# Two begun products of four pairs in place of two plain feature tiles at the start of the second feed forward

## The chip, the cores and the metric

One Trainium2 chip, one of its cores. The metric is the device time of one execution in microseconds; three executions of the kernel before gave 1340.26, 1340.63 and 1341.62 us, median 1340.63. Engines are named as in the profile: PE is TensorE (PEld its weight load), DVE is VectorE, ACT is ScalarE, POOL is GpSimd, SP is SyncE, whose queue issues the transfers. "Start" of an instruction is its place in the timeline, in us from the first instruction of the profiled execution.

## The reference

A decoder layer on 512 tokens of width 1024, all in fp32: a feed forward, token mixing, and a second feed forward. Only the last seam matters here.

```
def swiglu(x, w_gu, w_down):
    g, u = jnp.split(x @ w_gu, 2, axis=-1)
    return (jax.nn.silu(g) * u) @ w_down
...
h = h + rmsnorm(y, mix_post_w[l])                     # y: token mixing, y @ w_out
h = h + 0.5 * rmsnorm(swiglu(rmsnorm(h, ffn2_pre_w[l]), ffn2_w_gu[l], ffn2_w_down[l]), ffn2_post_w[l])
```

`w_gu` has 2 x 2816 columns: 22 feature tiles of 128 gate columns (g) and 128 up columns (u).

## The kernel before

**Numbers in two parts.** PE multiplies in a fast fp32 form. Each operand is split into a high part (`hi`, a rounding by ACT) and a low part (`lo`, the rest, a subtraction by DVE), and each product is three matmuls: hi·hi, hi·lo, lo·hi. So every weight piece of 128x512 elements costs one ACT and one DVE instruction before PE can use it (`split`, `wsplit`).

**Plain tiles and pairs.** The transposed, normalized tokens lie in `xhi[0]`, `xhi[1]` (the two halves of the 1024 inputs) with their low parts. The 512 tokens are four tiles t = 0..3 of 128; tiles 0 and 1 are the first token half, 2 and 3 the second. A plain feature tile (`gu_plain`) takes gate and up columns as they are: 8 slices x 3 matmuls x 2 column sets x 2 token halves = 96 matmuls with 256 moving columns. A pair (`pair`) takes the same gate and up columns as a 2 x 2 block product (input halves by token halves) with seven products in place of eight. Each product (`product`) is 12 matmuls of 256 columns, 84 in all. It pays for this on DVE. On the weight side there are sums s1, s2, s4 (a fourth, s3, is made by an accumulating transfer). On the token side there are the combinations t1..t4, made once by `combine`, which needs tile t of the second half with tile t - 2 of the first. Which operand a product needs:

```
self.xop = {1: q(0, 0), 2: q(1, 0), 3: q(1, 1), 4: self.xc["t4"], 5: self.xc["t1"], 6: self.xc["t2"], 7: self.xc["t3"]}
```

Products 1 and 2 read only the first token half; 3 reads the second half; 4 to 7 read the combinations t4, t1, t2, t3, which need both halves.

**The seam.** `out_proj` multiplies by `w_out` token tile by token tile, and per tile does the post norm (square on ACT, row factor `v` on DVE, power on POOL, two updates of h on DVE) and spawns `prenorm`: squares, factor, two scalings on DVE (line 204 before, 207 after), eight PE transposes into `px`, the splits into `xhi`, `xlo`, copies of the transposes kept for `combine`, and for t >= 2 `combine` itself. Tile 3 is the last, so its scaling ends the post norm chain of the whole seam.

Before, `ffn` of the second feed forward takes f = 0 and f = 1 as plain tiles (`early2=2, plain2=2`). It does both in the first token half, then one product of the pair f = 2 (`pair_begin`), and then both in the second token half. Then come the pairs, 20 of them, f = 2..21, with the `down` products of finished features between them (from f = 2 on, since the first chunk of `CHUNKS2` is 2 features).

**What sets the order.** The code is written in one order; a list scheduler places each engine's instructions by its own estimates, within dependences and pool sizes (18 split weights `w`, 5 `sum`, 4 `st`, 2 `sh`, 5 PSUM banks `ps`, 3 `px`). Each engine then works its own list strictly in order, and so does the SP queue. In names, the number behind a tile is its buffer.

Of the kernel before, what the change touches and what calls it, by code (L numbers as in the profile page):

```python
# [45 lines left out]

LAT = dict(comb=1.0, mem0=3.5, mem1=8.0, mem2=1.5, hg=1.5, hgx=6.0, hg1=6.0, hg2=11.0, hg3=6.0, hg4=6.0, dil0=4.0, exp=2.0, dil1=9.0, dil2=5.0,
           dil3=3.0, norm=8.0, mnorm=5.0, mload=10.0, start=0.1, step=2.0, keep=2.0)
PLAN = dict(early1=2, plain1=2, early2=2, plain2=2)
HALVES = (slice(0, 512), slice(512, 1024))  # L50


class Layer:
# [3 lines left out]
    def __init__(self, ctx, tc):  # L57
        self.tc, self.nc = tc, tc.nc
        nc = self.nc
        pool = lambda n, b, **k: ctx.enter_context(tc.tile_pool(name=n, bufs=b, **k))  # L60
        self.const = pool("const", 1)
        self.wpool = pool("wpool", NW)
        self.stage = pool("stage", NST)
        self.res = pool("res", 1)
        self.slots = pool("slots", NSLOT)
        self.small = pool("small", 4)
        self.ps = pool("ps", 5, space=PSUM)
        self.px = pool("px", 3, space=PSUM)
# [22 lines left out]
        self.ordered = 0  # L91

        self.strict = False

# [118 lines left out]
    def prenorm(self, src, gain, t, lat, raw):  # L213


        nc = self.nc
        ts = slice(t * P, (t + 1) * P)
        pts = []

        def keep(hf):  # L220
            raw[t, hf] = self.slot((P, 4, P))
            nc.scalar.copy(raw[t, hf], pts[hf])

        wait = self.strict and t < 2
        for x in self.normed(src, gain, lat, self.psum if self.strict and t == 1 else self.paux):
            if isinstance(x, float):
                yield x
                continue
            hf = len(pts)
            pts.append(x)  # L230
            self.split(self.xhi[hf][:, :, ts], self.xlo[hf][:, :, ts], x)
            if not wait and (t < 2 or hf == 0):
                keep(hf)
        if wait:
            def later():
                yield LAT['keep']
                keep(0)
                keep(1)
            self.spawn(later())
        if t < 2:  # L240
            return
        yield from self.combine(t, raw, pts, lat == LAT['norm'] and t == 2)
# [67 lines left out]
                out += [(hi[:, i, :], lo[:, i, :]) for i in range(per)]  # L310
        return out

    def wops(self, w, c1, c2, by_load):

        st = self.load(w, 0, KD, c1, P)
        a11, a12 = st[:, 0:4, :], st[:, 4:8, :]
        a22 = self.stage.tile([P, 4, P], F32, tag="st2", bufs=2, name=f"sh{self.uid()}")
        quarter = lambda h: w.rearrange("(k p) c -> p k c", p=P)[:, 4 * h:4 * h + 4, c2:c2 + P]  # L320
        self.bring(a22, quarter(1))
        sums, ops = {}, {}

        def new_sum():
            return self.wpool.tile([P, 4, P], F32, tag="sum", bufs=NSUM, name=f"sum{self.uid()}")

        if "s1" not in by_load:
            a21 = sums["a21"] = new_sum()
            self.bring(a21, quarter(0))
        for n, x in (("s1", a22), ("s3", a11)):  # L330
            if n in by_load:
                u = new_sum()
                self.bring(u, quarter(0))
                self.nc.gpsimd.dma_start(out=u, in_=x, accum_op=ALU.add)
                sums[n] = u
# [24 lines left out]
        def operand(j):  # L360
            if j not in ops:
                if j == 6:
                    total("s4")
                ops[j] = self.wsplit({1: a11, 2: a12, 4: a22}.get(j) if j in (1, 2, 4) else total({3: "s4", 5: "s1", 6: "s2", 7: "s3"}[j]))
            return ops[j]
        return get

    def pairs(self, specs, by_load=lambda i: ()):
# [24 lines left out]
    def product(self, out, ops, j, first=True):  # L393
# [3 lines left out]
        for k in range(4):  # L397
# [2 lines left out]
            mm(out, lhsT=lh, rhs=rl, start=False, stop=False, skip_group_check=True)  # L400
            mm(out, lhsT=ll, rhs=rh, start=False, stop=k == 3, skip_group_check=True)  # L401
            self.tick(3 * 0.1095)

    def pair_begin(self, ops):

# [179 lines left out]
    def ffn(self, w_gu, w_down, w_post, ready, reload, after, chunks, early, plain, last=False):  # L585


        nc = self.nc
# [4 lines left out]
        pairs = self.pairs([(w_gu, f * P, DFF + f * P) for f in range(plain, NF)], lambda i: ("s1", "s3")[i < 4:])  # L593

        def swiglu(sg, su, act):
            nc.scalar.activation(sg, sg, AF.Silu)
# [1 line left out]
            self.split(act[0], act[1], sg)  # L598

        def gu(ops, act):  # L600
            a, u, c, d, v = self.pair(ops)
            sg, su = self.slot(), self.slot()
            nc.scalar.copy(sg[:, :HT], a)
# [37 lines left out]
        if not resumed:  # L641
            self.open(ready, gw, uw, new_act, gu_mm, gu_act, heads, early)
            tasks = [[], ready.tasks]
        else:
            tasks.append(ready[0]())
        for i in range(early if resumed else 0):
            heads.append([[next(gw), next(uw)], new_act()])
            if i == 0:
                tasks.append(ready[1]())
        for i in range(early if resumed else 0):  # L650
            for j in range(2):
                if i == 0:
                    self.need(tasks[0][j])
                heads[i][0][j] = self.wcol(heads[i][0][j], i >= 2)
        self.strict = False
        begun = None
        for i in range(2):
            if i == 1 and resumed:
                begun = self.pair_begin(next(pairs))
            self.need(*tasks[i])  # L660
            for w, act in heads if i or resumed else ():
                gu_plain(w, act, slice(i * HT, (i + 1) * HT))
        f0, before, ws = 0, None, []
        for n in chunks:
            act = []
            for j in range(n):
# [6 lines left out]
                else:  # L673
# [610 lines left out]
def layer_kernel(ctx, tc, a, nbias, hmask, out):  # L1284
# [59 lines left out]
    def store(h, t):  # L1344
        for c, n in ((0, 512), (512, 256), (768, 256)) if t == NT - 1 else ((0, 512), (512, 512)):
# [2 lines left out]

    h1, h2 = spill("h1"), spill("h2")
    ready = L.ffn(a["ffn1_w_gu"][0], a["ffn1_w_down"][0], a["ffn1_post_w"][0], Source,  # L1350
                  reload(lambda t, hf: x[t * P:(t + 1) * P, HALVES[hf]]), follow(h1, a["mix_pre_w"][0]), CHUNKS1, PLAN['early1'], PLAN['plain1'])
    z = L.mixing(a, ready, nbias)
    ready = L.out_proj(z, a["w_out"][0], a["mix_post_w"][0], reload(lambda t, hf: h1[t][hf]), follow(h2, a["ffn2_pre_w"][0]))
    L.ffn(a["ffn2_w_gu"][0], a["ffn2_w_down"][0], a["ffn2_post_w"][0], [lambda: ready[:2], lambda: ready[2:]], reload(lambda t, hf: h2[t][hf]), store, CHUNKS2, PLAN['early2'], PLAN['plain2'], True)


def constants():
# [39 lines left out]
```

## Time and profile before

| What | Value |
|---|---|
| median of 3 executions | 1340.63 us (1340.26 to 1341.62) |
| span of the profiled execution | 1338.3 us; of its own time the page gives no other number |
| PE busy | 1326.2 us, 99% of the span |
| DVE, ACT, POOL busy | 78%, 56%, 7% |
| granted TensorE clock, mean | 0.999 |
| end of `out_proj` on PE / first plain product | 984.69 us |
| first matmul of what is left of pair f = 2 | 1010.30 us |

The span runs from the first to the last instruction; the median of the timed executions is 2.3 us above it. A busy PE is told from the starts of matmuls: their shown durations overlap.

### The profile page before, as it was taken

What the parts mean: (1) busy time and instruction counts of PE and PEld (TensorE: products, weight loads), DVE (VectorE), ACT (ScalarE), POOL (GpSimd) and SP (SyncE); (2) the same over time, 40 slices, a digit from 0 to 9 for tenths busy, and PEclk for the clock granted to TensorE, in tenths of its full rate; (3) what the DMA queues carried; (4) which work ended last, traced back from release to release, by engine and by line L of the source; (5) the groups of instructions that cost most, each with busy time, mean ns of one, the idle gap of its engine ahead of it and who ended that gap; (6) DMA issues with size and microseconds to landing.
All of it is one profiled execution on the core that took longest, in us unless ns stands there. A gap on an engine that the chain in (4) does not pass through costs nothing.

```text
span 1338.3 us, 24332 instructions
## 1 busy us (share of the span) xinstructions
PE 1326.2 (99%) x9228; PEld 1234.5 (92%) x9228; DVE 1044.0 (78%) x1979; ACT 754.1 (56%) x1557; POOL 87.3 (7%) x116
## 2 busy tenths in 40 slices
PE   9999999999999999999999999999999999999997
PEld 8999999999898988899899999999899999999996
DVE  7987777687897975699769968898588877777765
ACT  7764554465566764455665755566366644445541
POOL 1011110010100000000000000000011111111100
PEclk9999999999999999999999999999999999999999
DMA  9586556565525335334223333334645766555513
GB/s 252 150 203 164 144 147 166 126 161 184 166 66 158 111 95 177 121 106 127 64 80 111 112 87 96 103 98 150 202 111 158 187 164 154 142 143 155 145 64 126
DMA packets 238611, 183.14 MB, mean 137 GB/s; under 512 B 11129, under 2 KB 200990, under 8 KB 238494
## 3 DMA queue, kind: packets, MB, share of 16 engines
q1 hardware_dynamic: 223702, 159.49, 39.7%
q0 software_dynamic: 10368, 18.88, 8.5%
q10 hardware_dynamic: 4424, 3.22, 0.8%
q8 instruction: 72, 1.18, 0.4%
q14 instruction: 45, 0.37, 0.1%
HBM read 153.21 MB, written 9.47 MB: 122 GB/s over the span
## 4 chain that ended last, share of the span: by engine, by line
PE 65%; DVE 2%; DMA 1%; ACT 0%; issue 0%; POOLq 0%; DVEq 0%; ACTq 0%
PE ps L381 17%; PE ps L399 12%; PE ps L400 12%; PE ps L401 12%; PE px L381 7%; PE px L386 4%; PE px L390 1%; DVE w L168 1%; DVE s L168 0%; DMA sh<-in_w_in_dram 0%; DMA sum<-in_w_in_dram 0%; DVE s L736 0%; DVE s L1042 0%; DVE st L992 0%; ACT s L832 0%
## 5 line engine op out<-in xcount | busy, mean ns | idle before, releaser
L173 ACT ACTIVATE w<-sum 128x512 fp32r<-128x512 f32 x288 | 180.5, 631 | 208.6 <-PE ps L400 180.3
L168 DVE TENSOR_TENSOR w<-sum,w 128x512 fp32r<-128x512 f32 x288 | 197.0, 687 | 79.6 <-ACT w L173 77.6
L400 PE MATMUL ps<-xlo,w 128*128 128x256 f32 x864 | 245.0, 284 | 0.0
L399 PE MATMUL ps<-xhi,w 128*128 128x256 f32 x864 | 244.9, 283 | 0.0
L401 PE MATMUL ps<-xhi,w 128*128 128x256 f32 x864 | 244.5, 283 | 0.0
L173 ACT ACTIVATE w<-st 128x512 fp32r<-128x512 f32 x240 | 150.2, 630 | 119.0 <-PE ps L400 87.7
L168 DVE TENSOR_TENSOR w<-st,w 128x512 fp32r<-128x512 f32 x248 | 168.6, 687 | 33.6 <-ACT w L173 30.8
L381 PE MATMUL px<-s,s 128*128 128x512 f32 x816 | 193.0, 390 | 0.0
L168 DVE TENSOR_TENSOR s<-s,s 128x256 f32<-128x256 f32 (+3 forms) x317 | 176.5, 562 | 13.8 <-ACT s L173 3.1
L381 PEld LDWEIGHTS px<-s,s 128*128 128x128 f32 x816 | 150.6, 188 | 29.9 <-DVE s L168 0.4
L399 PEld LDWEIGHTS ps<-xhi,w 128*128 128x128 f32 x864 | 165.5, 192 | 2.1
L400 PEld LDWEIGHTS ps<-xlo,w 128*128 128x128 f32 x864 | 165.5, 192 | 2.0
L401 PEld LDWEIGHTS ps<-xhi,w 128*128 128x128 f32 x864 | 165.5, 192 | 0.0
L168 DVE TENSOR_TENSOR sum<-sum,st 128x512 f32<-128x512 f32 x176 | 120.2, 686 | 7.0 <-DMA st<-in_w_in_dram 2.5
L168 DVE TENSOR_TENSOR s<-s,ps 128x256 f32<-128x256 f32 (+1 forms) x195 | 93.0, 477 | 28.2 <-PE ps L381 22.2
L399 PE MATMUL ps<-t3hi,w 128*128 128x256 f32 x288 | 82.9, 288 | 0.0
L399 PE MATMUL ps<-t1hi,w 128*128 128x256 f32 x288 | 82.2, 285 | 0.0
L399 PE MATMUL ps<-t4hi,w 128*128 128x256 f32 x288 | 82.2, 285 | 0.0
L400 PE MATMUL ps<-t4lo,w 128*128 128x256 f32 x288 | 81.9, 284 | 0.0
L400 PE MATMUL ps<-t3lo,w 128*128 128x256 f32 x288 | 81.8, 284 | 0.0
L401 PE MATMUL ps<-t1hi,w 128*128 128x256 f32 x288 | 81.5, 283 | 0.0
L400 PE MATMUL ps<-t2lo,w 128*128 128x256 f32 x288 | 81.5, 283 | 0.0
(198 smaller groups left out, 2965.8 us busy)
## 6 DMA issues: line engine op xcount, KB each, us to landing
st<-in_ffn_w_gu_dram SPq DMA_DIRECT2D x48, 512.0 KB, 4.8
st<-in_w_in_dram SPq DMA_DIRECT2D x48, 512.0 KB, 3.7
st<-in_ffn_w_down_dram SPq DMA_DIRECT2D x44, 512.0 KB, 4.0
sum<-in_ffn_w_gu_dram SPq DMA_DIRECT2D x80, 256.0 KB, 3.3
sh<-in_ffn_w_gu_dram SPq DMA_DIRECT2D x40, 256.0 KB, 3.3
sum<-st POOLq DMA_DIRECT2D x40, 256.0 KB, 3.4
sum<-sh POOLq DMA_DIRECT2D x32, 256.0 KB, 3.6
sum<-in_w_in_dram SPq DMA_DIRECT2D x32, 256.0 KB, 3.0
```

What stands on the lines that cost most here:

```text
L168: ins = self.nc.vector.tensor_tensor(out=out, in0=a, in1=b, op=op)
L173: self.pin(self.nc.scalar.activation(hi, src, AF.Copy))
L381: self.pin_pe(mm(out, lhsT=lhs[l], rhs=rhs[r], start=a, stop=b))
L386: self.nc.tensor.matmul(out, lhsT=lhsT, rhs=rhs, start=start, stop=stop, **k)
L390: self.pin_pe(self.nc.tensor.transpose(out, in_, self.ident))
L399: mm(out, lhsT=lh, rhs=rh, start=first and k == 0, stop=False, skip_group_check=True)
L400: mm(out, lhsT=lh, rhs=rl, start=False, stop=False, skip_group_check=True)
L401: mm(out, lhsT=ll, rhs=rh, start=False, stop=k == 3, skip_group_check=True)
```

## The change

The second feed forward has no plain tile any more (`early2=0, plain2=0`), so all 22 features are pairs. In the first token half it does products 1 and 2 of the first four pairs (`begun2=4`, `pairs_begin`, in groups of two), each pair keeping its result of product 1 (`cp`) and of 1 + 2 (`sg`, the first half of the gate). When the second half comes, `pair_rest` does the five others in the order 7, 5, 6, 3, 4. The weights of the four pairs are loaded in two steps: at first only the 8 slices of gate columns (`st`), and the up columns (`sh`, and twice into `sum`, one of them with the accumulating transfer) when `more` is called. Since no plain tile reads the first input half of the second token half, that split (`xhi[0]`, `xlo[0]` of t = 2, 3) is left out (`whole`). The first feed forward has `begun1=0` and the same instructions as before.

```
-PLAN = dict(early1=2, plain1=2, early2=2, plain2=2)
+PLAN = dict(early1=2, plain1=2, begun1=0, early2=0, plain2=0, begun2=4)
...
-            self.split(self.xhi[hf][:, :, ts], self.xlo[hf][:, :, ts], x)
+            if self.whole or t < 2 or hf == 1:
+                self.split(self.xhi[hf][:, :, ts], self.xlo[hf][:, :, ts], x)
...
+    def pairs_begin(self, group):
+        out = []
+        for ops in group:
+            a, cp = self.psum((P, HT)), self.slot()
+            self.product(a, ops, 1)
+            self.nc.scalar.copy(cp[:, :HT], a)
+            out.append((ops, cp, self.slot(), a))
+        for ops, cp, sg, a in out:
+            self.product(a, ops, 2, False)
+            self.nc.scalar.copy(sg[:, :HT], a)
+        return [x[:3] for x in out]
+
+    def pair_rest(self, ops, cp):
...
+        c, d, b = (self.psum((P, HT)) for _ in range(3))
+        self.product(d, ops, 7)
+        nc.scalar.copy(p7, d)
+        self.product(c, ops, 5)
+        nc.scalar.copy(v, c)
+        self.product(b, ops, 6)
+        self.tt(u, cp[:, :HT], b, ALU.add)
+        self.tt(v, p7, v, ALU.subtract)
+        self.product(c, ops, 3, False)
+        self.product(d, ops, 4, False)
+        return u, c, d, v
...
+        first = [self.wops(w_gu, f * P, DFF + f * P, ("s3",), True) for f in range(plain, plain + begun)]
+        pairs = self.pairs([(w_gu, f * P, DFF + f * P) for f in range(plain + begun, NF)], lambda i: ("s1", "s3")[i < 4 - begun:])
...
-        begun = None
+        half = []
         for i in range(2):
-            if i == 1 and resumed:
-                begun = self.pair_begin(next(pairs))
             self.need(*tasks[i])
             for w, act in heads if i or resumed else ():
                 gu_plain(w, act, slice(i * HT, (i + 1) * HT))
+            if i == 0:
+                for j in range(0, begun, 2):
+                    half += self.pairs_begin(first[j:j + 2])
+        for x in first[:2]:
+            x.more()
+        ahead = first[2:]
...
-                        gu(begun or next(pairs), act[-1])
-                        begun = None
+                        gu(half.pop(0) if half else next(pairs), act[-1])
+                        if ahead:
+                            ahead.pop(0).more()
```

How the order moves, at two places. First PE, at the transposes of the last token tile (`px2592`, `px2594` before, `px2593`, `px2595` after; they read `s2553`, `s2554`, the two scaled halves of tile 3) and at the first matmul that reads the second token half. Before:

```order
L381 MATMUL ps2591_12419<-xlo0_90,w2583_12319 128x256
L381 MATMUL ps2591_12419<-xhi0_88,w2584_12320 128x256
L390 MATMUL px2592_12423<-ident_81,s2553_12271 128x128 x4
L390 MATMUL px2594_12432<-ident_81,s2554_12273 128x128 x4
L381 MATMUL ps2591_12419<-xhi0_88,w2583_12319 128x256
...
L401 MATMUL ps2607_12495<-xhi0_88,w2610_12498 128x256
L381 MATMUL ps2611_12517<-xhi0_88,w2571_12295 128x256
```

After:

```order
L412 MATMUL ps2586_12395<-xhi0_88,w2589_12398 128x256
L401 MATMUL px2593_12422<-ident_81,s2553_12269 128x128 x4
L401 MATMUL px2595_12429<-ident_81,s2554_12271 128x128 x4
L410 MATMUL ps2567_12289<-xhi1_89,w2577_12336 128x256
...
L412 MATMUL ps2586_12395<-xhi1_89,w2600_12457 128x256
L410 MATMUL ps2611_12496<-t3hi_96,w2613_12498 128x256
L410 MATMUL ps2610_12495<-t1hi_92,w2615_12516 128x256
```

Before, 75 of the 96 plain matmuls of the first half stand ahead of the transposes, and behind the half and one product (`ps2607`) come plain matmuls on the tokens themselves. After, the four products 1 (48 matmuls) stand ahead of the transposes, the four products 2 behind them, and then comes `t3hi`, a combination.

Second DVE, from behind the scaling of tile 3 to the subtraction that makes t3 of tile 3 (`s2597<-s2593,px2594` before, `s2598<-s2594,px2595` after). Before:

```order
L168 TENSOR_TENSOR s2539_12236<-s2507_12079,s2537_12227 128x512
...
L168 TENSOR_TENSOR s2541_12238<-s2509_12088,s2540_12237 128x512
L168 TENSOR_TENSOR xlo0_90<-px2592_12423,xhi0_88 128x4x128
L168 TENSOR_TENSOR xlo1_91<-px2594_12432,xhi1_89 128x4x128
L168 TENSOR_TENSOR t4lo_99<-s2541_12238,t4hi_98 128x4x128
L168 TENSOR_TENSOR s2595_12439<-s2515_12124,s2593_12430 128x512
L254 SCALAR_TENSOR_TENSOR s2596_12440<-s2595_12439,px2594_12432 128x512
L168 TENSOR_TENSOR s2597_12441<-s2593_12430,px2594_12432 128x512
```

After:

```order
L171 TENSOR_TENSOR s2539_12234<-s2507_12079,s2537_12225 128x512
L171 TENSOR_TENSOR w2622_12556<-sum2617_12533,w2621_12555 128x512
...
L171 TENSOR_TENSOR w2624_12572<-sh2601_12478,w2623_12571 128x512
L171 TENSOR_TENSOR s2541_12236<-s2509_12088,s2540_12235 128x512
L171 TENSOR_TENSOR w2636_12609<-sum2606_12489,w2635_12608 128x512
L171 TENSOR_TENSOR sum2640_12644<-sum2605_12487,st2564_12283 128x512
L171 TENSOR_TENSOR t4lo_99<-s2541_12236,t4hi_98 128x4x128
L171 TENSOR_TENSOR s2596_12436<-s2515_12124,s2594_12427 128x512
L171 TENSOR_TENSOR w2638_12627<-sum2605_12487,w2637_12626 128x512
L258 SCALAR_TENSOR_TENSOR s2597_12437<-s2596_12436,px2595_12429 128x512
L171 TENSOR_TENSOR s2598_12438<-s2594_12427,px2595_12429 128x512
```

Between the first row shown and the last stand, with both, 15 rows before and 17 after. Five of the 17 prepare weights of the begun pairs (`w2622`, `w2624`, `w2636`, `sum2640`, `w2638`); before, two of the 15 are 256-column rows of the plain tiles (gate times up, and its low part), and one more is `xlo0` of tile 3, which is left out now.

More of the change, by code (lines that the diff above doesn't have):

```diff
@@ L91, in __init__ @@
         self.ordered = 0
+        self.whole = True
         self.strict = False
@@ L311, in rows, with wops, more @@
         return out
-    def wops(self, w, c1, c2, by_load):
+    def wops(self, w, c1, c2, by_load, later=False):
         st = self.load(w, 0, KD, c1, P)
         a11, a12 = st[:, 0:4, :], st[:, 4:8, :]
-        a22 = self.stage.tile([P, 4, P], F32, tag="st2", bufs=2, name=f"sh{self.uid()}")
         quarter = lambda h: w.rearrange("(k p) c -> p k c", p=P)[:, 4 * h:4 * h + 4, c2:c2 + P]
-        self.bring(a22, quarter(1))
         sums, ops = {}, {}
+        a21 = a22 = None
         def new_sum():
             return self.wpool.tile([P, 4, P], F32, tag="sum", bufs=NSUM, name=f"sum{self.uid()}")
[L327 to L335, printed above, removed]
+        def more():
+            nonlocal a21, a22
+            a22 = self.stage.tile([P, 4, P], F32, tag="st2", bufs=2, name=f"sh{self.uid()}")
+            self.bring(a22, quarter(1))
+            if "s1" not in by_load:
+                a21 = sums["a21"] = new_sum()
+                self.bring(a21, quarter(0))
+            for n, x in (("s1", a22), ("s3", a11)):
+                if n in by_load:
+                    u = new_sum()
+                    self.bring(u, quarter(0))
+                    self.nc.gpsimd.dma_start(out=u, in_=x, accum_op=ALU.add)
+                    sums[n] = u
+        if not later:
+            more()
         def total(n):
@@ L365, in operand @@
             return ops[j]
+        get.more = more
         return get
@@ L583, in open, with ffn @@
         self.spawn(rest(2)), self.spawn(rest(3))
-    def ffn(self, w_gu, w_down, w_post, ready, reload, after, chunks, early, plain, last=False):
+    def ffn(self, w_gu, w_down, w_post, ready, reload, after, chunks, early, plain, begun, last=False):
         nc = self.nc
@@ L592, in ffn @@
         uw = self.col_tiles(w_gu, DFF, plain)
-        pairs = self.pairs([(w_gu, f * P, DFF + f * P) for f in range(plain, NF)], lambda i: ("s1", "s3")[i < 4:])
+        first = [self.wops(w_gu, f * P, DFF + f * P, ("s3",), True) for f in range(plain, plain + begun)]
+        pairs = self.pairs([(w_gu, f * P, DFF + f * P) for f in range(plain + begun, NF)], lambda i: ("s1", "s3")[i < 4 - begun:])
         def swiglu(sg, su, act):
@@ L600, in gu @@
         def gu(ops, act):
-            a, u, c, d, v = self.pair(ops)
-            sg, su = self.slot(), self.slot()
-            nc.scalar.copy(sg[:, :HT], a)
+            if isinstance(ops, tuple):
+                ops, cp, sg = ops
+                u, c, d, v = self.pair_rest(ops, cp)
+                su = self.slot()
+            else:
+                a, u, c, d, v = self.pair(ops)
+                sg, su = self.slot(), self.slot()
+                nc.scalar.copy(sg[:, :HT], a)
             self.tt(sg[:, HT:], u, c, ALU.add)
@@ L644, in ffn @@
         else:
-            tasks.append(ready[0]())
+            tasks += [ready[0](), ready[1]()]
         for i in range(early if resumed else 0):
             heads.append([[next(gw), next(uw)], new_act()])
-            if i == 0:
-                tasks.append(ready[1]())
         for i in range(early if resumed else 0):
@@ L1350, in layer_kernel @@
     ready = L.ffn(a["ffn1_w_gu"][0], a["ffn1_w_down"][0], a["ffn1_post_w"][0], Source,
-                  reload(lambda t, hf: x[t * P:(t + 1) * P, HALVES[hf]]), follow(h1, a["mix_pre_w"][0]), CHUNKS1, PLAN['early1'], PLAN['plain1'])
+                  reload(lambda t, hf: x[t * P:(t + 1) * P, HALVES[hf]]), follow(h1, a["mix_pre_w"][0]), CHUNKS1, PLAN['early1'], PLAN['plain1'], PLAN['begun1'])
     z = L.mixing(a, ready, nbias)
+    L.whole = PLAN['early2'] > 0
     ready = L.out_proj(z, a["w_out"][0], a["mix_post_w"][0], reload(lambda t, hf: h1[t][hf]), follow(h2, a["ffn2_pre_w"][0]))
-    L.ffn(a["ffn2_w_gu"][0], a["ffn2_w_down"][0], a["ffn2_post_w"][0], [lambda: ready[:2], lambda: ready[2:]], reload(lambda t, hf: h2[t][hf]), store, CHUNKS2, PLAN['early2'], PLAN['plain2'], True)
+    L.ffn(a["ffn2_w_gu"][0], a["ffn2_w_down"][0], a["ffn2_post_w"][0], [lambda: ready[:2], lambda: ready[2:]], reload(lambda t, hf: h2[t][hf]), store, CHUNKS2, PLAN['early2'], PLAN['plain2'], PLAN['begun2'], True)
 def constants():
```

3 lines of the change are left out of this document (added).

## The prediction

> **What bounds the kernel now.** I read the page's span and busy shares first, then PE's waits, then windows around the seam, and last the timelines of PE, DVE and ACT there.
>
> ```profile
> span 1338.3 us, 24332 instructions
> PE 1326.2 (99%) x9228; PEld 1234.5 (92%) x9228; DVE 1044.0 (78%) x1979; ACT 754.1 (56%) x1557; POOL 87.3 (7%) x116
> ...
> PE ps L1303 <- POOL ident masks.py:199: 1.4, 1, 1.4
> ...
> PE ps L381 <- DVE xlo L168: 0.3, 1, 0.3
> ```
>
> PE is busy for all but about 12 us, and the longest single wait that it has on anyone is 1.4 us, at the very start. So a matmul taken away is time gained, as long as PE still finds the next one ready. The windows show the four stretches of the seam (columns: length, then busy us of each engine, the granted clock, DMA share and rate): the plain tiles' first half, one product and the second half, the rest of the pair f = 2, and then the pairs alone.
>
> ```profile
> 984.69:997.06 12.37, 12.37 (x106) 12.37 (x104) 9.39 (x17) 6.55 (x14) 1.93 (x3) 1.00 0.48 136
> 997.06:1010.46 13.40, 13.37 (x112) 13.17 (x111) 13.33 (x25) 10.32 (x23) 0.00 (x0) 1.00 0.09 24
> 1010.46:1019.10 8.64, 8.64 (x74) 8.64 (x73) 7.89 (x17) 4.70 (x11) 0.89 (x1) 1.00 0.81 224
> 1070.00:1302.00 232.00, 232.00 (x1614) 217.62 (x1612) 169.65 (x295) 115.08 (x223) 22.41 (x26) 1.00 0.54 139
> ```
>
> In the second stretch DVE is busy 13.33 of 13.40 us: PE is covered there by plain matmuls whose weights were already split, while DVE makes the combinations t1..t4. That cover is what the change takes away.
>
> **What goes: 24 matmuls.** Two plain features are 2 x 96 = 192 matmuls of 256 columns, two pairs are 2 x 84 = 168. Their price is the distance of starts on PE:
>
> ```profile
> 984.69 0.28 PE L381 MATMUL ps<-xhi,w 128*128 128x256 f32 x1
> ...
> 993.68 1.04 PE L390 MATMUL px<-ident,s 128*128 128x128 f32 x8
> 994.47 0.36 PE L381 MATMUL ps<-xhi,w 128*128 128x256 f32 x1
> ...
> 997.06 0.28 PE L399 MATMUL ps<-xhi,w 128*128 128x256 f32 x1
> 997.18 0.28 PE L400 MATMUL ps<-xlo,w 128*128 128x256 f32 x1
> ...
> 1010.30 0.28 PE L399 MATMUL ps<-t2hi,w 128*128 128x256 f32 x1
> ...
> 1018.94 0.86 PE L381 MATMUL px<-s,s 128*128 128x512 f32 x3
> ```
>
> 72 matmuls lie between 1010.30 and 1018.94, so one is 0.12 us, and 24 are 2.9 us. That is the gain if PE never waits.
>
> **What is added: a wait for the last combination.** I reckon it as one time, R, when PE can start the first matmul on t3 (the `t3hi` row of the order). At 1010.30 PE had 72 matmuls of its pair and 19 pairs of 84 to do, 1668. At R it has four rests of 60 and 18 pairs of 84, 1752, and the `down` products are the same. 84 more at 0.12 are 10.1 us, so the end moves by R + 10.1 - 1010.30 = R - 1000.2.
>
> Were all data there, PE would come to it 96 matmuls and eight transposes behind 984.69: 11.5 and 0.8 us (993.68 to 994.47), R = 997.0 and the end 3.2 us earlier (2.9 for the matmuls, the rest for the short stall that the waits list has as 0.3). But t3 needs tile 3, and that comes from the norm chain, which was paced like this:
>
> ```profile
> 979.36 1.41 DVE L204 SCALAR_TENSOR_TENSOR s<-s,r,s 128x512 f32<-128x512 f32 x2 [0.73 <-POOL r L195]
> ...
> 986.23 0.69 DVE L168 TENSOR_TENSOR s<-ps,s 128x512 f32<-128x512 f32 x1
> 986.83 0.20 DVE L192 TENSOR_SCALAR v<-ss,ss 128x1 f32<-128x1 f32 x1
> 987.78 1.42 DVE L266 SCALAR_TENSOR_TENSOR s<-s,r,s 128x512 f32<-128x512 f32 x2 [0.74 <-POOL r L195]
> 990.05 0.21 DVE L192 TENSOR_SCALAR v<-ss,ss 128x1 f32<-128x1 f32 x1 [0.85 <-ACT s L186]
> 990.99 1.42 DVE L204 SCALAR_TENSOR_TENSOR s<-s,r,s 128x512 f32<-128x512 f32 x2 [0.73 <-POOL r L195]
> 992.32 0.68 DVE L168 TENSOR_TENSOR s<-s,s 128x512 f32<-128x512 f32 x1
> ...
> 1001.19 0.68 DVE L168 TENSOR_TENSOR s<-s,px 128x512 f32<-128x512 f32 x1
> 1001.79 0.69 DVE L168 TENSOR_TENSOR t1lo<-s,t1hi 128x512 fp32r<-128x512 f32 x1
> 1002.39 0.69 DVE L168 TENSOR_TENSOR t2lo<-s,t2hi 128x512 fp32r<-128x512 f32 x1
> 1002.99 0.69 DVE L168 TENSOR_TENSOR t3lo<-s,t3hi 128x512 fp32r<-128x512 f32 x1
> ```
>
> Even before, the subtraction that makes t3 of tile 3 starts at 1001.19. ACT's side of it:
>
> ```profile
> 985.50 0.60 ACT L186 ACTIVATE s<-ps 128x512 f32<-128x512 f32 x1
> ...
> 988.63 0.63 ACT L186 ACTIVATE s<-s 128x512 f32<-128x512 f32 x1 [2.43 <-DVE s L266]
> 989.16 0.19 ACT L186 ACTIVATION_READ_ACCUMULATOR s<-s 128x1 f32 x1
> 989.29 0.63 ACT L186 ACTIVATE s<-s 128x512 f32<-128x512 f32 x1
> ...
> 1001.90 0.63 ACT L173 ACTIVATE t3hi<-s 128x512 fp32r<-128x512 f32 x1
> ```
>
> Does the scaling of tile 3 move? Before, nine 512-column rows stand on DVE between the end of tile 2's scaling (979.36 + 1.33) and the row at 986.23; now eight (`xlo0` is gone, and the weight rows are as many less one, plus one sum), 0.6 us less, though ACT's square, which cannot start before PE has ended `out_proj` near 984.9, gives back a little. Between the two squares at 988.63 and 989.29 ACT now has one weight rounding (`w2619`), at most as long as the row at 1001.90, 0.63 us. The two about cancel: I keep 992.32 as the time at which DVE is through with the scaling.
>
> Now the queue behind it: 16 rows stand between that and the t3 subtraction, all of 512 columns at 0.60 us from start to start (1001.19, 1001.79, 1002.39): 9.7 us, start 1002.0, against 1001.19 before. ACT's rounding began 0.71 us behind that start and took 0.63; with a tenth for the hand-over R = 1002.0 + 0.71 + 0.63 + 0.1 = 1003.4. The end moves by 1003.4 - 1000.2 = +3.2 us.
>
> On PE this appears as a wait at the transposes (48 matmuls end at 984.69 + 5.8 = 990.5, tile 3 is scaled at 991.7 and 992.4), one at the first product 2, which overwrites a bank that ACT has to copy first and ACT stands behind t1 of tile 2, and the rest ahead of t3: about 6 us in all, of which none adds to R, since DVE's queue sets it.
>
> [...]
>
> **The other terms.** The accumulating transfers move: two of them, `sum` from `st`, now stand on POOL's queue ahead of the first row factor `r` instead of behind the sixth. They wait for `st` loads issued on SP at 936.6 to 942.7, and the first factor is due at 956.6, so they are through long before; cost 0. Two loads of `st` (512 KB) leave the SP queue between the stores of h; loads of `sum` and `sh` for the third and fourth pair take their places behind those stores, the last of them behind a `down` load that waits for DVE.
>
> ```profile
> 936.61 6.04 SPq L155 DMA_DIRECT2D st<-in_ffn_w_gu_dram  x3
> ...
> 956.60 0.56 POOL L195 TENSOR_TENSOR r<-v,mhalf 128x1 f32<-128x1 f32 x1 [396.86 <-DVE v L192]
> ...
> sum<-st POOLq DMA_DIRECT2D x40, 256.0 KB, 3.4
> ...
> sum<-st POOLq DMA_DIRECT2D x4, 256.0 KB, 5.2
> ```
>
> The fourth pair's accumulated sum is the late one: load near 1006, 3 us, then 3.4 us (page, whole run) to 5.2 us (issues of 890 to 1030), so 1012 to 1016, while PE comes to that pair at R + 3 x 7.2 + 2.7 = 1027.7 with DVE and ACT rows in between. I take 0; with the longer landing ACT's list is held up and up to 2 us may come on top. Behind R DVE has 21.6 us of PE work to hide three rests: up to the last weight of the third pair it is 27 rows from `t3lo` on, at most 0.60 each, 16.2 us from 1002.6, done by 1018.8 against a need at 1003.4 + 14.4 + 5.8 = 1023.6. So PE waits no more. Silu's table load goes to a place where ACT waits anyway. The skipped split (2 ACT, 2 DVE rows) is in the counts. The last stretches, 1070 on, have DVE busy 73% beside a full PE and stay.
>
> Sum: the span goes from 1338.3 to 1341.5 us. The timed median is 2.3 us above the span; I add the same: 1340.63 + 3.2 = 1343.8 us, +0.24%. A difference under 0.2% (2.7 us) is what a measurement of this kernel can hardly tell from none.
>
> **Rivals.** Hidden in part (chance 0.24): R comes 0.5 to 2 us sooner, because the scaling of tile 3 really gains the 0.6 us and the rows run closer. Nearest row: if t3 came as early as before (ACT at 1001.90, so R 1002.6) the end moves +2.4 us, 1343.0. Against it stand five weight rows in DVE's list.
>
> Faster (0.06): DVE is not the pace because the combinations of tile 3 overtake the weights; then the 24 matmuls count, 1340.63 - 3.2 = 1337.4. It decides where R is under 997.5: ten of the 16 rows would have to be gone. The order speaks against it.
>
> More waits behind R (0.12): the late sum above, or acts of the first two pairs not ready at the first `down`; +1 to +2.5 us more, 1345 to 1346.3.
>
> The clock (0.06): PE has run at a granted 1.00 in all windows shown, with no wait above 1.4 us; now it has single waits of about 2 us, 6 in 13. If the grant fell to half for the first two products behind R, their 24 matmuls would take 2.9 us more: 1346.7. No row shows a fall. [...]
>
> **How the numbers follow.** My forecast, 1343.8, has 0.52, with 1343.0 to 1344.8 as its own range. The range 1341.9 to 1346.4 takes in most of the part hidden and of the waits behind R, and leaves out the faster case and the clock. Faster by over 0.2%: the faster rival, 0.06. Within: the part hidden (0.24) and the low edge of the forecast, together 0.30. Slower: the rest, 0.64.
>
> **What would show it.** PE rows 24 fewer; in PE's waits new entries on DVE and ACT at the seam, about 6 us, the last and longest ahead of `t3hi`, 2 to 3 us; t3's rounding at 1002.7; the first `down` at R + 21.6 = 1025.0; no PE wait behind it. I am wrong if `t3hi` begins before 999, or if PE waits again behind 1010.

## The result, and the profile after

| | before | after |
|---|---|---|
| median | 1341.12 us (6 runs, 1340.26 to 1343.05) | 1350.27 us (6 runs, 1346.94 to 1352.61) |
| ratio, 95% interval | | 1.0065 [1.0054, 1.0076] |
| profiled execution: time, span | span 1338.3 us | 1350.46 us, span 1348.7 us |
| forecast | | 1343.8 us (1341.9 to 1346.4) |

The change made the kernel 9.2 us slower. The forecast had the direction, and about a third of the size. From the page after:

```profile
span 1348.7 us, 24331 instructions
PE 1325.5 (98%) x9204; PEld 1232.3 (91%) x9204; DVE 1050.9 (78%) x1993; ACT 758.1 (56%) x1565; POOL 90.8 (7%) x120
```

The 24 matmuls are gone (9228 to 9204) and PE is busy 0.7 us less, yet the span is 10.4 us longer. The list of PE's waits shows where it stands still (waiter, releaser: us in all, times, longest):

```profile
PE ps L410 <- ACT s L451: 2.8, 2, 2.5
PE px L401 <- DVE s L207: 2.2, 3, 1.1
PE ps L410 <- ACT s L422: 2.0, 2, 1.3
PE ps L410 <- ACT t3hi L176: 1.9, 1, 1.9
...
PE ps L392 <- ACT s L176: 1.0, 1, 1.0
...
PE ps L410 <- ACT s L439: 0.8, 1, 0.8
```

Their places in PE's timeline, from the first transposes of token tile 0 (the first row below is the kernel before, the rest is after; 963.64 to 965.57, so everything from here on is 1.93 us late to begin with):

```profile
963.64 0.60 PE L390 MATMUL px<-ident,s 128*128 128x128 f32 x4
...
965.57 1.03 PE L401 MATMUL px<-ident,s 128*128 128x128 f32 x8
...
993.67 1.29 PE L401 MATMUL px<-ident,s 128*128 128x128 f32 x8 [1.14 <-DVE s L207]
996.25 0.39 PE L410 MATMUL ps<-xhi,w 128*128 128x256 f32 x1 [1.29 <-ACT s L422]
1000.12 0.39 PE L410 MATMUL ps<-xhi,w 128*128 128x256 f32 x1 [0.74 <-ACT s L422]
1005.11 0.39 PE L410 MATMUL ps<-t3hi,w 128*128 128x256 f32 x1 [1.87 <-ACT t3hi L176]
1034.83 0.38 PE L410 MATMUL ps<-xhi,w 128*128 128x256 f32 x1 [0.80 <-ACT s L439]
1048.95 0.58 PE L410 MATMUL ps<-xhi,w 128*128 128x256 f32 x1 [2.48 <-ACT s L451]
1049.32 0.41 PE L411 MATMUL ps<-xlo,w 128*128 128x256 f32 x1
1049.54 0.41 PE L412 MATMUL ps<-xhi,w 128*128 128x256 f32 x1
```

The first four waits are the seam, much as forecast: the transposes of tile 3, a copy ahead of product 2 in each group (the forecast had the first group's alone), and t3. The last two, 30 and 44 us behind t3, are not in the forecast. And behind the last one matmuls stand 0.21 us apart instead of 0.12: the clock has fallen. The windows there (length, busy us of PE, PEld, DVE, ACT, POOL, then the granted clock):

```profile
1046.00:1048.00 2.00, 0.47 (x4) 0.26 (x3) 1.62 (x4) 2.00 (x5) 0.23 (x1) 1.00 0.67 118
1048.00:1050.00 2.00, 1.05 (x5) 1.06 (x6) 2.00 (x5) 1.98 (x6) 0.00 (x0) 0.73 0.09 13
1050.00:1052.00 2.00, 2.00 (x11) 2.00 (x11) 2.00 (x4) 0.86 (x3) 0.00 (x0) 0.50 0.83 219
1052.00:1054.00 2.00, 2.00 (x17) 2.00 (x17) 1.97 (x5) 1.10 (x3) 0.00 (x0) 0.92 1.01 305
```

For about 3.4 us, 1048.95 to 1052.31, the grant is 0.50. 15 matmuls take 3.36 us there instead of 1.80: 1.6 us.

What the last wait hangs on is told by the chain of waits (start, length, what):

```profile
1024.02 4.62 DMA sum<-sh
1028.64 0.61 DVE w L171
1029.27 6.87 DMA sh<-in_ffn_w_gu_dram
1036.18 0.49 issue
1036.67 2.31 DMA sum<-sh
1038.98 0.34 DVE s L171
1039.33 4.30 issue
1043.63 0.70 DVE sum L171
1044.44 0.54 ACT w L176
...
1048.11 0.52 ACT w L176
1048.63 0.27 ACT s L451
1048.95 0.58 PE ps L410
```

Read it from the DVE split at 1028.64 on, which is the last to read an `sh` buffer (the transfer of the first row lands only at 1030.39 and does not hold it up). Only behind that split can SP load the next `sh`, which takes 6.87 us to land; only then can POOL issue the next accumulating transfer `sum<-sh` (1036.67); it lands at 1043.55, 6.9 us from its issue, and DVE makes the next sum at 1043.63 (the 4.30 us called "issue" are DVE's wait for that landing). ACT, idle for 5.5 us, then has eight instructions in a row, roundings and two copies, and behind them the copy of PSUM (L451) for which PE waits. The change put this second transfer there: `i < 4 - begun` with `begun` = 4 gives every pair from index 4 on both sums by transfer; before, pairs 2 to 5 made s1 on DVE.

The 0.8 us wait at L439 is of another kind. There ACT's list has the rounding of a sum that both kernels make by transfer (`sum<-st`, issued at 1025.12, landed at 1033.81) ahead of the copy. In sums4 below, that sum lands as late (1033.26), but its rounding stands behind the copy, and PE does not wait.

Counted by starts, with the matmuls of both kernels numbered back from the last, PE is 1.93 us behind the kernel before at the transposes of tile 0, 5.00 us behind t3, 6.05 us behind the wait at L439 and 10.27 us from the end of the half clock to the last matmul. So of the span's 10.4 us 1.9 were lost ahead of the seam, 3.1 at t3, 1.1 at L439 and 4.2 at L451 with the half clock. (By starts a wait costs some 0.3 us more than the list says: the list counts from the shown end of the matmul before, and the first two starts behind a wait stand 0.22 us apart.)

### The profile page after: what moved, and what is told of

It is laid out like the page before. It is cut to its first block, busy times and chain, and to the rows that moved or that the text cites. A ratio compares the mean times of both kernels' runs of the same rounds, so it can differ in the third digit from the quotient of the medians.

```text
span 1348.7 us, 24331 instructions
## 1 busy us (share of the span) xinstructions
PE 1325.5 (98%) x9204; PEld 1232.3 (91%) x9204; DVE 1050.9 (78%) x1993; ACT 758.1 (56%) x1565; POOL 90.8 (7%) x120
## 4 chain that ended last, share of the span: by engine, by line
PE 59%; DVE 3%; DMA 2%; ACT 1%; issue 1%; POOL 0%; POOLq 0%; DVEq 0%; ACTq 0%
PE ps L392 14%; PE ps L410 11%; PE ps L411 11%; PE ps L412 11%; PE px L392 7%; PE px L397 4%; DVE w L171 1%; PE px L401 1%; DVE s L171 1%; DMA sum<-sh 1%; DMA sh<-in_ffn_w_gu_dram 1%; DMA st<-in_ffn_w_gu_dram 0%; ACT w L176 0%; DVE sum L171 0%; DMA sh<-in_w_in_dram 0%
## 5 line engine op out<-in xcount | busy, mean ns | idle before, releaser
L176 ACT ACTIVATE w<-sum 128x512 fp32r<-128x512 f32 x296 | 185.1, 631 | 211.9 <-PE ps L411 180.8
L171 DVE TENSOR_TENSOR w<-sum,w 128x512 fp32r<-128x512 f32 x296 | 202.3, 686 | 80.7 <-ACT w L176 79.2
L410 PE MATMUL ps<-xhi,w 128*128 128x256 f32 x888 | 252.9, 285 | 5.7 <-ACT s L451 2.8
L411 PE MATMUL ps<-xlo,w 128*128 128x256 f32 x888 | 252.4, 284 | 0.0
L412 PE MATMUL ps<-xhi,w 128*128 128x256 f32 x888 | 251.9, 284 | 0.0
L171 DVE TENSOR_TENSOR w<-st,w 128x512 fp32r<-128x512 f32 x244 | 165.7, 687 | 34.2 <-ACT w L176 31.5
L171 DVE TENSOR_TENSOR s<-s,s 128x512 f32<-128x512 f32 (+3 forms) x321 | 179.2, 564 | 15.4 <-ACT s L176 4.3
L410 PEld LDWEIGHTS ps<-xhi,w 128*128 128x128 f32 x888 | 170.8, 192 | 8.8 <-ACT s L451 3.3
L411 PEld LDWEIGHTS ps<-xlo,w 128*128 128x128 f32 x888 | 170.8, 192 | 2.0
L412 PEld LDWEIGHTS ps<-xhi,w 128*128 128x128 f32 x888 | 170.8, 192 | 0.0
L341 POOL DMA_DIRECT2D sum<-st x42 | 36.6, 871 | 797.2 <-DVE t3lo L171 383.5
L410 PE MATMUL ps<-t1hi,w 128*128 128x256 f32 x296 | 84.5, 285 | 0.0
L412 PE MATMUL ps<-t1hi,w 128*128 128x256 f32 x296 | 83.8, 283 | 0.0
```

The source lines that it names most:

```text
L171: ins = self.nc.vector.tensor_tensor(out=out, in0=a, in1=b, op=op)
L176: self.pin(self.nc.scalar.activation(hi, src, AF.Copy))
L410: mm(out, lhsT=lh, rhs=rh, start=first and k == 0, stop=False, skip_group_check=True)
```

## Experiments

Each was timed beside the kernel before; ratios are to that. sums4, hold, before_sums and mix ran on one chip, mix3, mix3_pre, sums4_pre and sums4_fill on a second, sums2, fill2 and hold_fill on a third, and hold_fill3 later on the first again, so these are compared across groups by their ratios.

**sums4: without the second accumulating transfer at pairs 4 to 7.**

```
-lambda i: ("s1", "s3")[i < 4 - begun:]
+lambda i: ("s1", "s3")[i < 4:]
```

> The changed kernel, but pairs 4 to 7 make their first sum on DVE, as pairs 2 to 5 did before the change; one accumulating transfer each instead of two. Theory (the second accumulating transfer comes late at pairs 4 and 5, holds up DVE and then ACT, and PE waits for a copy of a bank): the waits of 0.8 us (L439) and 2.5 us (L451) behind t3 go, and with them the slow clock that follows the long one (1.7 us): 1350.3 - 5.0 = 1345.3 us. Rival (the loads on SP come late because the buffers of sum and sh come free late, whoever adds): a wait of 2 us or more stays in that place, 1349 to 1351 us. Second rival (the slow clock is a late effect of the seam's own waits): the waits go, the clock still falls under 0.9 somewhere in the 60 us behind t3, 1347 us.

Measured: 1346.62 us, ratio 1.0042 [1.0029, 1.0056]; 5.5 us above the kernel before where the change itself was 9.2. PE's waits on L439 and L451 are gone:

```profile
PE px L401 <- DVE s L207: 2.0, 2, 1.1
PE ps L410 <- ACT s L422: 2.0, 2, 1.3
...
PE ps L410 <- ACT t3hi L176: 1.9, 1, 1.9
```

The late sums are shown as a cause, and the rival that the loads alone are late falls. But the clock fell all the same, now right behind the wait for t3, as the second rival had it:

```profile
1004.00:1006.00 2.00, 2.00 (x10) 2.00 (x11) 2.00 (x4) 0.42 (x2) 0.00 (x0) 0.58 0.11 33
1006.00:1008.00 2.00, 2.00 (x13) 2.00 (x12) 2.00 (x4) 0.94 (x2) 0.00 (x0) 0.57 0.42 128
```

**before_sums: the transfer alone, in the kernel before.**

```
-lambda i: ("s1", "s3")[i < 4:]
+lambda i: ("s1", "s3")[i < (2 if last else 4):]
```

> The kernel before, with one thing of the change: pairs from index 4 on take both sums by accumulating transfer (before: from index 6 on); seam and begun pairs as before. Theory (two accumulating transfers for pairs 4 and 5 are late by themselves): PE waits 1 to 3 us between 1018 and 1045, 1342 to 1344.5 us. Rival (they are late only where the seam has moved the loads on SP): no wait, within 0.7 us of the kernel before.

Measured: 1340.76 us, ratio 0.9998 [0.9989, 1.0007], and no wait of PE behind the seam. The rival holds: a second accumulating transfer at pairs 4 and 5 costs nothing by itself. Here POOL issues the two at 1017.19 and 1026.87 us, in the change at 1024.02 and 1036.67: it costs where the new seam has made them late. That it is the loads of the four begun pairs ahead of them that do so is read from the order; no run shows it alone.

**sums2: the change, with only pairs 4 and 5 put back** (`i < (2 if begun else 4)`).

> The changed kernel, but only pairs 4 and 5 make their first sum on DVE, as they did before the change; pairs 6 on have two accumulating transfers as in both kernels. Theory (it is these two pairs' second transfer that is late): the same as sums4, waits behind t3 gone, 1346.6 us within 0.7. Rival (the queue is late from the seam on, and the next pair with two transfers pays): a wait of 1 us or more at pair 6 or 7, 1048 to 1070, 1348 us or more.

Measured: 1345.71 us, ratio 1.0030 [1.0019, 1.0041], on another chip; within the interval of sums4. In the profile the wait at L451 is 0.2 us and the one at L439 is gone. It is these two pairs.

**hold: the weights of later products behind t4 of the last tile.** The token combinations should overtake five weight rows on DVE.

```
+            if i and begun:
+                self.opened2 = (self.last_low, self.last_hi)
...
         self.product(b, ops, 6)
+        self.opened = self.opened2
```

`opened2` is t4 of tile 3; from the second line on, weights stand behind it.

> The changed kernel, but the weights of the last two products of the first rest and of everything behind them stand on DVE and ACT behind t4 of the last tile. Theory (t3 is set by the rows in DVE's queue): 5 of 16 rows go from between the scaling and the t3 subtraction, 5 x 0.60 = 3.0 us: the first matmul on t3hi comes 36.5 us behind the first transpose of tile 0 instead of 39.5 (965.57 to 1005.11), and the time is 1350.3 - 3.0 = 1347.3 us. Rival (the weights held back are then missing): t3hi comes 3 us sooner, but PE waits for weights in the first two rests and the end moves by 1 us or less, 1349.5 to 1351 us. Second rival (ACT or the transposes set t3): t3hi moves by under 1 us.

Measured: 1350.56 us, ratio 1.0069 [1.0056, 1.0081]: no gain. t3hi came 38.5 us behind the first transposes of tile 0 instead of 39.5, 1.0 us of the 3.0: with the rows out of the way DVE waited for ACT instead, for t4's rounding and the copy of a transpose, which stands behind copies of products (the second rival). Behind t3 a weight held back was then missing (L414), and the late sum still held up a copy in `pair` (L469). Lines are 2 to 3 higher here:

```profile
PE ps L412 <- ACT s L424: 2.5, 2, 1.3
PE ps L412 <- ACT s L469: 2.4, 1, 2.4
...
PE ps L414 <- DVE w L171: 0.8, 1, 0.8
```

**mix: one plain feature and two begun pairs**, with `i < 4` as in sums4.

```
-early2=0, plain2=0, begun2=4
+early2=1, plain2=1, begun2=2
```

> Between the two kernels: one plain feature in token halves as cover, two pairs begun in the first half instead of four, and pairs 3 to 6 make the first sum on DVE. 12 matmuls fewer than before (12 x 0.12 = 1.4 us), 12 more than in the changed kernel. Theory (what the change lost is the cover up to R): the 48 plain matmuls of the second half (5.8 us) end near R = 1003.2, PE's wait ahead of t3hi is under 0.7 us, and with no wait behind it the end comes 0 to 1.4 us before the kernel before: 1339.7 to 1341.1 us; if the 1.9 us that the changed kernel had lost ahead of the seam belong to the change, 1341.6 to 1343 us. Rival (the rows of the plain feature's own product stand in DVE's queue and push t3 back): the wait ahead of t3hi is 1.5 us or more, 1343 us or more.

Measured: 1343.16 us, ratio 1.0018 [1.0009, 1.0027], the nearest to the kernel before, but not faster. Its cover stood in the wrong place. t3 was waited for no longer; instead PE came to the plain tile's second half too soon, behind 72 matmuls where the kernel before had 108 (24 of the missing 36 stand behind the wait), and waited for `xhi` of tile 3:

```profile
999.70 0.58 PE L392 MATMUL ps<-xhi,w 128*128 128x256 f32 x1 [2.87 <-ACT xhi L176]
```

**mix3: three begun pairs in place of two** (`begun2=3`), to put 24 more matmuls ahead of that half.

> As mix, but three pairs begun in the first half instead of two: 24 more matmuls (2.9 us) stand ahead of the plain feature's second half, which waited 2.87 us for xhi of the last tile. Theory (cover): that wait goes, and with it the half clock behind it, 1343.2 - 2.9 - 1.2 = 1339.1 us; 12 matmuls fewer than the kernel before, so 0 to 2 us ahead of it. Rival (more weight rows ahead of the last tile's chain push it back by as much): a wait of 1.5 us or more stays, 1342 us or more.

Measured: 1346.44 us, ratio 1.0040 [1.0028, 1.0052]: worse, and the expectation missed. That wait is gone, but others of 1.8 us (the transposes of tile 0, on DVE), 1.2 us (a transpose, on an ACT copy) and 2.1 us (L422) came. Why the norm chain was late already at tile 0 I have not settled.

**mix3_pre: mix3, the first weights held behind the last operand of `out_proj`** (`self.opened` set to that split as the second feed forward begins).

> mix3 with the first weights held until the last operand of the output projection is split: only two DVE sums that wait for loads move, to 30 and 50 rows later. Theory: the 0.4 us that PE waited for DVE near 946 in mix goes: 0.3 to 0.8 us below mix3, 1338.4 us. Rival: they stand where DVE is idle anyway, the same as mix3 within 0.3 us.

Measured: 1345.88 us, ratio 1.0035 [1.0023, 1.0047]; not told apart from mix3. The same hold on sums4, for the 1.0 us wait near 944:

> sums4 with the first pairs' weights held until the last operand of the output projection is split: on ACT one weight rounding that waits for a load then stands behind that split instead of ahead of it, on DVE two sums that wait for loads stand some 30 and 50 rows later. Theory (the wait of PE near 944 in the changed kernel, 1.0 us, is that split standing behind a load that lands late): the wait can't come, and the runs lose it where they had it: 0.3 to 1.0 us less than sums4, 1345.6 to 1346.3 us. Rival (it is the loads' own pace): no difference, within 0.3 us of sums4.

Measured: 1346.77 us, ratio 1.0035 [1.0023, 1.0047], against 1346.62 us. No gain. That wait, of 1.0 to 1.2 us, stood in the profiles of the change, hold, sums4_fill and fill2, and not in those of sums4, sums2, hold_fill and hold_fill3, which do the same there: it comes with the landing of a load that ACT rounds just ahead of what PE needs (issued at 937.31, 6.2 us to land in the change; 4.9 us in the kernel before, whose order is the same there, and in sums4), and I can't put it down to the change.

**sums4_fill: PE kept at work while it waits for t3.**

```
+        if not self.filled:
+            self.filled = True
+            with self.tc.issue_after(self.last_mm):
+                for i in range(14):
+                    nc.tensor.transpose(d[:, :P], self.ident, self.ident)
         self.product(d, ops, 7)
```

> sums4 with 14 transposes of the identity put on PE behind the last begun product, ahead of the first matmul on t1 to t3: they write a bank that the next product starts anew and change nothing of the result. They take 14 x 0.11 = 1.5 us of the 1.9 us that PE stands still there. Theory (the slow clock answers to PE standing still, and not to the matmuls that follow): no half clock in the seam, mean clock of the runs 0.998 to 0.999 instead of 0.996 to 0.998, 1346.6 - 1.5 = 1345.1 us, and less spread. Rival (half clock comes from something else, load of the chip or the earlier waits at 992 to 999): half clock as in sums4, 1346.6 us or 0.2 more.

Measured: 1344.25 us (11 runs), ratio 1.0024 [1.0016, 1.0033], 2.4 us below sums4; the mean granted clock of the runs rose from 0.9968 to 0.9976 (the kernel before: 0.9986). So with 14 transposes that compute nothing the kernel came out faster, though the two intervals just overlap and sums4 ran on another chip (sums4_pre, on the same one, took 1346.77 us). The profiled execution is one of the slower ones of it, 1345.83 us, and shows the half clock at another wait, behind the two of 1.1 and 1.3 us that were left unfilled:

```profile
994.00:996.00 2.00, 0.77 (x3) 0.77 (x4) 2.00 (x4) 2.00 (x6) 0.89 (x1) 0.63 0.03 8
996.00:998.00 2.00, 2.00 (x12) 2.00 (x11) 2.00 (x5) 0.50 (x1) 0.00 (x0) 0.50 0.76 131
998.00:1000.00 2.00, 2.00 (x11) 2.00 (x11) 2.00 (x4) 0.91 (x2) 0.00 (x0) 0.50 0.07 20
```

**fill2: that place filled too,** with 12 transposes behind those of tile 3.

> sums4_fill with 12 more transposes of the identity right behind the transposes of tile 3 (12 x 0.11 = 1.3 us, where PE waited 1.29 us for a copy), besides the 14 ahead of the first matmul on t1 to t3. What is left of PE's waits in the seam is 1.1 us ahead of the transposes of tile 3 and under 0.8 us later. Theory (half clock follows where PE stood still for some 2 us within a few us): no half clock in the profile, mean clock 0.998 to 0.999 in all runs, and 0.5 to 1 us below sums4_fill (1344.25), 1343.5 us, which leaves the cost of the late t3 alone, 3.2 us less what runs scatter. Rival (half clock comes where it did, whatever PE does): mean clock 0.996 to 0.998, 1344.3 us or more.

Measured: 1344.76 us beside a kernel before of 1342.23 on that chip, ratio 1.0027 [1.0016, 1.0037]: not told apart from sums4_fill, so the further 0.5 to 1 us was not seen. Nor is it told apart from sums2, which has the same seam without fill and ran on the same chip (1345.71 us, 1.0030): there, filling is worth 1 us at most by the medians. No half clock in the profiled execution between 960 and 1100; mean clock 0.9981 over 7 runs (sums2: 0.9974; the kernel before on that chip: 0.9981).

**hold_fill: fill2 with the hold.**

> fill2 with the hold of the second run: the weights of the last two products of the first rest and all later ones behind t4 of the last tile. There t3hi came 1.0 us sooner (38.5 us behind the first transpose of tile 0 instead of 39.5), and the gain was not seen behind a wait for a late sum and a half clock. Theory (the end follows t3 one to one where nothing waits behind it): 1.0 us below fill2, 1342.5 us. Rival (the 0.8 us wait at 1016 for a weight held back takes it): the same as fill2 within 0.3 us.

Measured: 1344.08 us, ratio 1.0019 [1.0009, 1.0029], mean clock 0.9985. It can't tell about t3: the 14 transposes kept PE until 39.5 us behind tile 0, so the products on t1 to t3 could not start sooner.

**hold_fill3: 3 transposes there instead of 14.**

> hold_fill with 3 instead of 14 transposes of the identity ahead of the first matmul on t3: in hold_fill those 14 themselves kept PE until 39.5 us behind the first transpose of tile 0, as late as without the hold, so that run could not tell. Theory (the end follows t3 one to one): t3hi at 38.3 to 38.6 us, 1.0 us below hold_fill: 1.2 us above the kernel before and its runs' scatter. Rival (weights held back are missing): a wait of 0.7 us or more within 25 us behind t3hi, the same as hold_fill.

Measured: 1345.86 us, ratio 1.0032 [1.0022, 1.0042]; no gain. PE began on t1 to t3 1.3 us sooner (38.3 us behind tile 0 instead of 39.5), and gave it back by the second rest, whose product 3 starts 51.57 us behind tile 0 against 51.16 in the change: the weights held back were missing, the rival of the expectation.

```profile
1013.61 0.38 PE L414 MATMUL ps<-t1hi,w 128*128 128x256 f32 x1 [0.25 <-DVE w L171]
1015.42 0.39 PE L414 MATMUL ps<-t2hi,w 128*128 128x256 f32 x1 [0.24 <-DVE w L171]
1016.72 0.28 PE L412 MATMUL ps<-xhi,w 128*128 128x256 f32 x1
```

No variant beat the kernel before.

## Why the prediction was right or wrong

**R, the start on t3: right.** With the 1.93 us of the start taken off, t3hi began at 1003.18 (forecast 1003.4), the t3 subtraction at 1001.8 (1002.0; row 1003.72) and the first `down` at 1024.9 (1025.0; row 1026.81). The scaling of tile 3 was through at 992.2 (992.32; row 994.10), and from there the 16 rows follow each other without a gap, as the sum had it:

```profile
994.10 0.68 DVE L171 TENSOR_TENSOR s<-s,s 128x512 f32<-128x512 f32 x1
...
1003.72 0.68 DVE L171 TENSOR_TENSOR s<-s,px 128x512 f32<-128x512 f32 x1
...
1026.81 2.91 PE L392 MATMUL px<-s,s 128*128 128x512 f32 x12
```

The waits in the seam were there, 5.0 us (about 6), the one ahead of t3 1.87 us (2 to 3). The end moved by 3.0 us through this by the forecast's own formula (1003.18 - 1000.2), 3.1 by starts (+3.2 forecast). Where the late sums are gone and the seam's waits are filled, the kernels are 3.1 us (sums4_fill), 2.5 us (fill2) and 1.9 us (hold_fill) above their kernel before by the medians, and 4.3 us in hold_fill3, where weights held back were missing. hold adds a limit: with five rows out of DVE's list t3 gained 1.0 us and not 3.0, since ACT's list is the next to hold it.

**The 24 matmuls at 0.12 us: right in number.** They are in R - 1000.2.

**Two terms set at nothing behind R: wrong; this is the step that failed.** "The other terms" priced the fourth pair's sum, up to 2 us, took 0, and ended with "So PE waits no more". The sums that came late were those of pairs 4 and 5, by a second accumulating transfer each, which the diff's `4 - begun` gave them and the working never priced. Taking it back took away waits of 0.8 and 2.5 us. The rival "more waits behind R" (0.12) had the kind and not the place; "no PE wait behind it" was the sentence that told it wrong. From the ratios, 1.0065 to 1.0042 with those transfers back on DVE, this was some 3 us.

**The clock at 0.06: wrong.** The rival had 24 matmuls at half clock behind R; it was 15, behind the late wait, 1.6 us and not 2.9. "No row shows a fall" was true of a kernel whose PE hardly waits, and it is no evidence on one that does. Between 960 and 1100 half clock is in the profiles of the change, sums4, sums4_pre, hold, mix, mix3 and sums4_fill. It is not in those of sums2 and mix3_pre, nor in the three others whose waits are filled (fill2, hold_fill, hold_fill3), nor in the two kernels without waits there. One stretch costs 1.6 us; from sums4 to sums4_fill the ratio fell by 0.0018, 2.4 us. The same wait before t3 was followed by half clock in sums4 (1.87 us) and not in the change (1.87 us) or in sums2 (1.86 us); the stretch of the change came behind its wait of 2.48 us.

No run here sets when the clock may fall, but the traces' record of the granted clock shows a grid. The stretch of the change is 3.413 us long in it. Within each trace the half-clock stretches begin a whole number of such lengths apart: in the change at 1048.92 and at 1345.88 us (the end of the program), 87.0 times that; in sums4 98.0, in hold 82.0, in mix 100.0, in mix3 99.0, in sums4_pre and sums4_fill 101.0 times. The full clock ahead of the first of them fits too: it lasted 1044.48 us in the change, 306.0 times 3.413, and 1327.79 us in the kernel before, 389.0 times. Lay out windows of 3.413 us from there (in a trace without an earlier stretch from the one at the end of the program), and add up the time that PE stands still in each:

| run | window, us | PE still, us | grant in the next window |
|---|---|---|---|
| the change | 1045.51 to 1048.92 | 2.46 | 0.50 |
| sums4 | 1000.90 to 1004.31 | 1.87 | 0.50 |
| sums4_fill | 991.10 to 994.51 | 1.75 | 0.50 |
| sums2 | 1000.70 to 1004.11 | 1.71 | 1.00 |
| mix3_pre | 997.06 to 1000.47 | 1.63 | 1.00 |
| the change, at t3 | 1001.14 to 1004.55 | 1.31 | 1.00 |

Between 940 and 1100 seven windows of the fourteen traces have 1.75 us or more, and the clock fell behind each of them; all others have 1.71 us or less, and it fell behind none, except that in sums4_fill it stayed at half for a second window, with 0.72 us of standing still in the first. So in these traces the fall went with the sum of the still time in one window, 1.75 us or more of its 3.413, and not with the longest wait. In the change the border at 1004.55 cut the wait for t3 in two, in sums4 the whole of it lay in one window: the same wait with and without a half clock, by luck of the phase.

**DVE rows 0.60 apart: right.** t3's start came 0.2 us from the sum by these: the 16 rows, 0.68 us long, took 9.62 us from the first start (994.10) to the t3 subtraction (1003.72), 0.60 each.

**Accumulating transfers ahead of the first row factor, cost 0: not contradicted.** They were issued by 946.5 (rows 944.07 and 945.61 on POOL), and the first factor came at 958.54. Of the 1.9 us that were lost ahead of the first transposes, 0.7 are there already at 717 us, long before the seam, and the rest is the wait near 944, which other executions of the same order lack. before_sums, with the order of the kernel before up to here, came to these transposes 1.30 us later than that kernel did, so much of the 1.9 can be scatter.

Adding up the ratios: 3 us for the late sums, 2.4 for PE's filled wait, 3.2 left, of 8.7. The intervals are about 0.0010 wide each way, so each part is sure to some 2 us; the profile's own sum (5.3 in the two late waits with the half clock, 3.1 at t3, 1.9 ahead) tells of one execution in another split.

## What to carry to other kernels

When a change moves the start of a stage, follow every buffer ring that is filled from there until it is in its old rhythm, not only the first wait: here a helper's index (`i < 4 - begun`) moved work from DVE to transfers that were harmless in the old order and 3 us in the new one. A matmul engine that never waited has also never shown what a wait does to its clock: where an edit trades matmuls for waits of 2 us, add up the still time of neighbouring waits over some 3.4 us, and price one half-clock stretch (1.6 us here) behind them where it comes near the 1.75 us that were enough here. If the wait can't be had away, matmuls that compute nothing may be cheaper than standing still: here they seemed worth 2 us on one chip and 1 us on another, within the scatter of the runs.

## What the runs showed of the hardware

The granted clock fell to 0.50 for about 3.4 us behind single PE waits of 1.87 us (sums4), 2.45 us (hold), 2.48 us (the change) and 2.87 us (mix), matmuls of 256 columns then standing 0.21 us apart instead of 0.12; it did not always fall (1.86 us in sums2). In sums4_fill two waits of 1.15 and 1.29 us with only eight transposes between them were enough, for 6.8 us. The falls of one trace lie on a grid of 3.413 us, and between 940 and 1100 they came behind exactly those windows of it in which PE stood still for 1.75 us or more (1.71 us or less: none). Part of the scatter of one kernel goes with the clock: the change took 1346.94 and 1350.46 us at a mean clock of 0.998 and 1352.61 us at 0.994.

An accumulating transfer of 256 KB landed 3.3 us behind its issue at 995.60 in the change, and 8.7 us behind its issue at 1025.12, where SP had issued four loads within 2 us (1023.87 to 1025.68).
